# A one-core hybrid decoder layer: a mask moved to a longer-lived pool, decay tiles allocated together and held behind a copy, and another order of the opening's tokens

## The chip, the core and the metric

The kernel runs on one core of a Trainium2 chip. Its time is the device time of one execution in microseconds (us). In the profile PE is the matrix engine, PEld its loading of weights, DVE, ACT and POOL are the vector, scalar and GpSimd engines, and SP issues nearly all DMAs (SPq is its queue). Each engine takes its instructions in a fixed order and waits at the first one whose inputs or buffers aren't ready.

## The reference

One decoder layer works on 1024 tokens of width 1024 in float32. A norm feeds one input projection, whose columns go to two groups of heads that run side by side; their outputs are joined, projected, added to the input, and an MLP follows.

```python
# group A: differential attention, 4 heads, two 64-wide softmax maps per head
s = jnp.einsum('bqhcd,bkhcd->bhcqk', qb, k) * scale
p = jax.nn.softmax(s, axis=-1)
a = p[:, :, 0] - lam * p[:, :, 1]
...
# group B: gated DeltaNet, 4 heads, chunks of 64
g = jnp.cumsum(g, axis=-1)
gdiff = g[..., :, None] - g[..., None, :]
decay = jnp.where(tri, jnp.exp(jnp.where(tri, gdiff, 0.0)), 0.0)
Lmat = jnp.where(strict, jnp.einsum('bhncd,bhnjd->bhncj', k_beta, k) * decay, 0.0)
sol = lax.linalg.triangular_solve(Lmat, rhs, left_side=True, lower=True, unit_diagonal=True)
...
def step(state, inp):      # scanned over the chunks
    v_new = u_c - jnp.einsum('bhcd,bhde->bhce', w_c, state)
    ...
    state = state * jnp.exp(g_last)[..., None, None] + jnp.einsum('bhcd,bhce->bhde', k_dec, v_new)
```

## The kernel before

A float32 matrix product is made of three passes in a narrower format: each operand is split into a high and a low part (hH and hL of the activations, wH and wL of the weights), and PE multiplies high by high, low by high and high by low. ACT makes the high part by a cast, DVE the low part by a subtraction. So every projection step is three matmuls on three neighbouring lines (L305 to L307 for the DeltaNet projections, L1391 to L1393 for the attention's queries and keys).

The work runs in this order.

- **Opening.** The tokens come in transposed, 128 at a time (`xT`, blocks tb of 0 to 7), and the gate projection `z` in two units of columns, u of 0 and 1. Its first blocks take the raw tokens (`z_raw`, L452); later blocks are scaled by their norm first (`z_scale_parts`). For that ACT sums squares, DVE and POOL make a root (`z_root`: nrt, nr), ACT a diagonal matrix (`z_diag`: dg), and PE spreads it over the partitions (`z_spread`: ps_r, L511). The order on all engines is written out by hand here (`manual_schedule`).
- **DeltaNet projections**, in the order keys, queries, values (`dn_proj(1)`, `dn_proj(0)`, `dn_proj(2)`), four heads in two halves each. A half's 24 matmuls end in a bank of a two-bank pool (pj), and ACT copies it away (`cp`, L763), which frees the bank. Weights come in 128x512 pieces (`load_unit`, `wraw`), in two buffers; a buffer is free when ACT has cast it and DVE has subtracted. Beside the keys, `decay(h, hf)` makes the matrix of decays: four ACT products each for rrh and rrl (L832), two matmuls into ps_e (L834, L835), an exponential.
- **Triangular inverses.** `invert()` inverts blocks of 32, and `horner` joins them to blocks of 128, two heads per call, four calls. A call multiplies ps_p (L909), masks it with `blk` into pb (DVE, L912), runs ps_h with 96, 64 and 32 columns (L917), each after what DVE or ACT made of the one before, and scales its result W (DVE, L925).
- **Scan and attention.** From here a planner interleaves the scan over chunks with the attention's projections (ps_qk) and then the attention itself, the output projection and the MLP. The scan reads parked keys and values into `pka` (SP, L1066, four DMAs a chunk), multiplies W by them (ps_A, L1107), applies the result (L1118), updates the state S, and for the second chunk takes the remainder `sr` (DVE, L1073) after a product with S (L1098).

The order of the instructions comes from a scheduler that simulates the program as it is written, except in the opening. Memory comes from pools that are stacked: `sp` lives through the scan, `gp` lies above it and is closed before the scan, whose pool `sb` is then opened in its place. A tile that takes over memory waits for the last reader of what lay there. In the kernel before, `blk` is in `gp`, and its memory lies under the first `pka`.

Of the kernel before, what the change touches and what calls it, by code (L numbers as in the profile page):

```python
# [9 lines left out]
F32 = mybir.dt.float32  # L10
# [8 lines left out]
P = 128  # L19
# [206 lines left out]
def tile_hymba_layer(  # L226
# [161 lines left out]
    def z_load(u, k):  # L388
        nc.sync.dma_start(wz[u][1][k // 2].rearrange("p k c -> p (k c)"), w_z[u, k // 2, :, 0:2 * UC])

    wz = [z_unit() for u in range(2)]
    for tb in range(2):
        xTs[tb] = n1.tile([P, KB, P], F32, tag="xT", name="xT", bufs=6)

    def x_piece(eng, tb, a, b):
        eng.dma_start(xTs[tb][:, a:b, :], x_cols[tb, :, a:b, :])

    z_load(0, 0)
    x_piece(nc.sync, 0, 0, 2)
    x_piece(nc.scalar, 0, 2, 4)  # L400
    z_load(0, 2)
    x_piece(nc.sync, 0, 4, KB)
    z_load(0, 4)
    z_load(0, 6)
    x_piece(nc.sync, 1, 0, KB)
    for k in range(0, KB, 2):
        z_load(1, k)
    dnw4 = n1.tile([P, 4, P], F32, name="dnw4")
# [69 lines left out]

    sums, roots, spreads, diags = {}, {}, {}, {}

    def z_weigh(tb, *at):
        for a, b in zip(at, at[1:]):
            V.tensor_tensor(xTs[tb][:, a:b, :], xTs[tb][:, a:b, :],
                            w1c[:, a:b].unsqueeze(2).broadcast_to([P, b - a, P]), ALU.mult)

    def z_hi(tb, i):
        S.copy(hH[:, cuts[i], tb * P:(tb + 1) * P], xTs[tb][:, cuts[i], :])
# [10 lines left out]
    def z_root(tb):  # L498

        r = roots[tb] = n1.tile([P, 1], F32, name=f"nr{tb}")  # L500
        rstd(r, sums[tb], 1.0 / DM, EPS, n1, "nrt", 1)
# [12 lines left out]
    def z_scale_parts(tb):  # L514
        sl = slice(tb * P, (tb + 1) * P)
        xT, last = xTs[tb], []
        for c in cuts:
            if tb < 2:
                V.tensor_tensor(xT[:, c, :], xT[:, c, :], spreads[tb].unsqueeze(1).broadcast_to([P, 4, P]), ALU.mult)
            else:  # L520
                for k in range(c.start, c.stop):
                    V.scalar_tensor_tensor(xT[:, k, :], xT[:, k, :], w1c[:, k:k + 1], spreads[tb], ALU.mult, ALU.mult)
            last.append(S.copy(hH[:, c, sl], xT[:, c, :]))
        yield
        for c in cuts:
            last.append(V.tensor_tensor(hL[:, c, sl], xT[:, c, :], hH[:, c, sl].bitcast(F32), ALU.subtract))
        yield last

    def z_scale(tb):
        return list(z_scale_parts(tb))[1]  # L530

    ones = gp.tile([P, P], F32, name="ones")
    V.memset(ones, 1.0)
    tri = sp.tile([P, P], F32, name="tri")
    gt_f = gp.tile([P, P], F32, name="gt_f")
    blk = gp.tile([P, P], F32, name="blk")
    caus_f = gp.tile([P, P], F32, name="caus_f")
    G.memset(caus_f, 0.0)
    G.affine_select(caus_f, caus_f, pattern=[[-1, P]], compare_op=ALU.is_ge, fill=-1.0e30,
# [9 lines left out]
    with tc.manual_schedule(engines={T.engine, V.engine, S.engine, G.engine}):  # L549

        pw = pm.tile([P, 512], F32, tag="pm", name="ps_w")
        for i in range(10):
            T.transpose(pw[:, 0:P], ident, ident)
        z_weigh(0, 0, 2, 4)
        z_round(0, 0)
        z_hi(0, 0)
        z_lo(0, 0)
        z_weigh(0, 4, KB)
        z = {(0, 0): z_raw(0, 0, pj, "pj")}
        z_round(0, 1)  # L560
        z_rest(0, 0)
        z_hi(0, 1)
        z_rest(0, 1)
        z_lo(0, 1)
        z_round(0, 2)
        z_rest(0, 2)
        z_weigh(1, 0, 4, KB)
        z_round(0, 3)
        z_rest(0, 3)
        z[1, 0] = z_raw(1, 0, pj, "pj")  # L570
        for i in range(4):
            z_round(1, i)
            z_rest(1, i)
            if i % 2 == 0:
                z_hi(1, i // 2)
        z_square(2)
        z_root(2)
        z_diag(2)
        z_lo(1, 0)
        z_lo(1, 1)  # L580
        z[0, 1] = z_ahead(0, 1, ph, "ph")
        z_spread(2)
        z_square(3)
        z_root(3)
        z_diag(3)
        G.tensor_scalar(dnw4[:, 0], dnw4[:, 0], 0.5, None, ALU.mult)
        G.tensor_copy(dnw4[:, 1:4], dnw4[:, 0:1].broadcast_to([P, 3, P]))
        dnw4 = dnw4.rearrange("p h e -> p (h e)")
        z[1, 1] = z_ahead(1, 1, ph, "ph")
        z_spread(3)  # L590
        z_scale(2)
        z_square(0)
        z_square(1)
        parts = z_scale_parts(3)
        next(parts)
        for tb in range(2):
            z_root(tb)
        next(parts)
        z_square(4)
        z_root(4)  # L600

        pools = {3: (pj, "pj"), 4: (ph, "ph"), 5: (pt_, "pt"), 6: (pj, "pj"), 7: (ph, "ph")}
        z[2, 0] = z_ahead(2, 0, pt_, "pt")
        z_gate(0, 0, z[0, 0], True)
        z_diag(4)
        z[2, 1] = z_mm(2, 1, pt_, "pt")
        z_gate(1, 0, z[1, 0], True)
        z_square(5)
        gates_due = {(3, 0): ((0, 1), (1, 1)), (3, 1): ((2, 0), (2, 1)), (4, 1): ((3, 0), (3, 1)),
                     (5, 0): ((4, 0), (4, 1)), (5, 1): ((5, 0),), (6, 0): ((5, 1),), (6, 1): ((6, 0),),  # L610
                     (7, 0): ((6, 1),), (7, 1): ((7, 0), (7, 1))}
        spread_at = {(3, 0): (4, 1), (3, 1): (5, 3), (4, 1): (6, 1), (5, 0): (7, 3), (5, 1): (0, 3), (6, 0): (1, 3)}
        for tb in range(3, NT):
            for u in range(2):
                nxt, at = spread_at.get((tb, u), (None, 0))
                z[tb, u] = z_mm(tb, u, *pools[tb], nxt, at)
                if nxt is not None:
                    parts = z_scale_parts(nxt)
                    if nxt == 5:
                        z_square(7)  # L620
                    next(parts)
                    if nxt in (4, 5):
                        b = {4: 5, 5: 7}[nxt]
                        z_root(b)
                        z_diag(b)
                    last = next(parts)
                    if nxt == 5:
                        mark = [marks[5], *last]
                for b, v in gates_due.get((tb, u), ()):
                    z_gate(b, v, z[b, v], b < 2)  # L630
                if (tb, u) == (3, 0):
                    z_square(6)
                    z_root(6)
                    z_diag(6)
                if (tb, u) == (3, 1):
                    z_diag(0)
                    z_diag(1)
# [110 lines left out]
    for cp in cps:  # L748
        V.memset(cp[:, 0:3], 0.0)

    def dn_proj(kind):
        for pr in range(2):
            with tc.issue_after(x_last.ins) if kind == 1 and pr == 0 else ExitStack():
                w = load_unit(w_units[4 + 2 * kind + pr])
            for hl in range(2):
                h = 2 * pr + hl
                u = 4 * kind + h
                cp = cps[hl]
                for hf in range(2):
                    ps = pj.tile([P, 512], F32, tag="pj", name="ps_dn")  # L760
                    trn(ps, w, hl * P, hf)
                    b = 512 * hf
                    S.copy(cp[:, 3 + b:3 + b + 512], ps)  # L763
                    y = ta("cy", 2)
                    S.activation(y, cp[:, 3 + b:3 + b + 512], AF.Copy, scale=pv[:, 36 + u:37 + u])  # L765
                    for wi in (2, 1, 0):
                        V.scalar_tensor_tensor(y, cp[:, wi + b:wi + b + 512], pv[:, 12 * wi + u:12 * wi + u + 1],  # L767
                                               y, ALU.mult, ALU.add)
                    if kind == 1:
                        th = ta("cth", 2)  # L770
                        S.activation(th, y, AF.Tanh, scale=0.5)
                        yield h, hf, y, th
                    else:
                        o = ta("cth" if hf else "k2", 2)
                        S.activation(o, y, AF.Silu)
                        yield h, hf, o
# [48 lines left out]
    dts = {}  # L825

    def decay(h, hf):
        rh, rl = ta("rrh", 1, F32R), ta("rrl", 1, F32R)
        for t, col in ((rh, ggh), (rl, ggl)):
            for c in range(4):  # L830
                i = cidx(h, 4 * hf + c)
                S.activation(t[:, c * P:(c + 1) * P], tri, AF.Copy, scale=col[:, i:i + 1])  # L832
        pse = ph.tile([P, 512], F32, tag="ph", name="ps_e")
        T.matmul(pse, gt_r, rh, start=True, stop=False)  # L834
        T.matmul(pse, gt_r, rl, start=False, stop=True)  # L835
        dtm = sa.tile([P, 512], F32, name=f"dtm{h}{hf}")
        S.activation(dtm, pse, AF.Exp)
        G.tensor_tensor(v4(dtm), v4(dtm), bc_mask(tri), ALU.mult)
        dts[h, hf] = dtm

    def invert():

# [12 lines left out]

    lt = {}
    for h, hf, y, th in skew(dn_proj(1)):
        decay(h, hf)
        k2 = ta("k2", 2)
        V.scalar_tensor_tensor(k2, th, 1.0, y, ALU.add, ALU.mult)  # L860
        park(h, hf, 0, k2)
# [1569 lines left out]
```

## Time and profile before

| | |
|---|---|
| median of 3 runs | 1207.59 us (1206.82 to 1209.14) |
| profiled execution | 1208.18 us |
| its span | 1206.5 us, 1.7 us less than its time |
| PE busy | 1195.2 us, 99% of the span |
| DVE, ACT, POOL busy | 854.1, 619.6, 143.0 us |
| mean granted clock of PE | 0.999 |

Rows of a timeline give start, duration, engine, line, operation, tile and inputs, the shape and the count, and in brackets how long the engine had been idle and what ended it. Matmuls overlap, so the cost of one is the distance from its start to the next one's start, not its duration. Rows of windows give the stretch, its length, the busy time and the number of instructions of PE, PEld, DVE, ACT and POOL, the granted clock of PE as a share of full speed, the share of the DMA engines and the GB/s.

### The profile page before, as it was taken

How to read it: one execution, taken by the hardware profiler on the slowest of the kernel's cores; microseconds unless marked ns; L12 is line 12 of the kernel's file. 1: busy time of each engine (PE TensorE's matmuls, PEld its weight loads, DVE VectorE, ACT ScalarE, POOL GpSimd, SP SyncE). 2: the span in 40 equal slices, each digit the busy share in tenths (PEclk: the TensorE clock that was granted, in tenths of full speed). 3: DMA queues.
4: the chain of work that ended last, by engine and by line, in shares of the span. 5: the costliest groups of instructions: out<-in, count | busy, mean ns of one | idle time of the engine just before them, and what ended most of it. 6: DMA issues, size and time to landing. Idle time of an engine off the chain costs nothing.

```text
span 1206.5 us, 17495 instructions
## 1 busy us (share of the span) xinstructions
PE 1195.2 (99%) x6183; PEld 998.0 (83%) x6183; DVE 854.1 (71%) x1655; ACT 619.6 (51%) x1226; POOL 143.0 (12%) x183
## 2 busy tenths in 40 slices
PE   9999999999999999999999999999999999999998
PEld 8978888878888777888888888888888888888887
DVE  6879897656677799886895655456669755786543
ACT  6588553424446666785664544445653333333330
POOL 2423210013322333011100000000000000000000
PEclk9999999999999999999999999999999999999999
DMA  9344654526755766213537443344489555423301
GB/s 352 95 120 122 173 161 88 126 80 217 221 165 156 215 182 187 62 40 116 172 118 249 176 156 125 137 174 174 157 280 386 189 209 194 139 87 105 140 35 70
DMA packets 163966, 191.56 MB, mean 159 GB/s; under 512 B 63160, under 2 KB 119720, under 8 KB 163880
## 3 DMA queue, kind: packets, MB, share of 16 engines
q1 hardware_dynamic: 160136, 180.72, 46.9%
q0 software_dynamic: 3456, 9.60, 2.2%
q8 instruction: 48, 0.79, 0.3%
q14 instruction: 38, 0.31, 0.1%
q10 hardware_dynamic: 288, 0.14, 0.0%
HBM read 129.43 MB, written 60.98 MB: 158 GB/s over the span
## 4 chain that ended last, share of the span: by engine, by line
PE 95%; DVE 1%; ACT 1%; DMA 1%; issue 0%; POOL 0%; SPq 0%; DVEq 0%; ACTq 0%
PE X L2001 5%; PE X L2003 5%; PE X L2002 5%; PE X L2330 4%; PE X L2329 4%; PE X L2328 4%; PE ps_dn L307 3%; PE ps_dn L305 3%; PE ps_dn L306 3%; PE ps_o L1644 3%; PE ps_sc L1551 3%; PE ps_qk L1391 3%; PE Y L2001 3%; PE Y L2003 3%; PE Y L2002 3%; PE ps_qk L1393 2%
## 5 line engine op out<-in xcount | busy, mean ns | idle before, releaser
L1880 ACT CAST hH<-ur 128x1024 fp32r<-128x1024 f32 x56 | 58.9, 1051 | 173.3 <-PE Y L2329 89.4
L1881 DVE TENSOR_TENSOR hL<-ur,hH 128x1024 fp32r<-128x1024 f32 x56 | 68.4, 1222 | 79.3 <-ACT hH L1880 79.3
L1881 DVE TENSOR_TENSOR op<-raw,op 128x1024 fp32r<-128x1024 f32 x48 | 58.7, 1223 | 73.6 <-PE X L2002 40.4
L2328 PE MATMUL X<-hH 128*128 128x512 f32 x224 | 87.1, 389 | 0.0
L2329 PE MATMUL X<-hL,hH 128*128 128x512 f32 x224 | 87.1, 389 | 0.0
L2330 PE MATMUL X<-hH,hL 128*128 128x512 f32 x224 | 87.1, 389 | 0.0
L305 PE MATMUL ps_dn<-hH,wH 128*128 128x512 f32 x192 | 75.9, 395 | 0.5 <-ACT cp L763 0.5
L307 PE MATMUL ps_dn<-hH,wL 128*128 128x512 f32 x192 | 75.3, 393 | 0.0
L306 PE MATMUL ps_dn<-hL,wH 128*128 128x512 f32 x192 | 75.3, 392 | 0.0
L1881 DVE TENSOR_TENSOR hL<-dw,hH 128x1024 fp32r<-128x1024 f32 x56 | 68.1, 1218 | 0.8 <-ACT hH L1880 0.7
L1880 ACT CAST op<-raw 128x1024 fp32r<-128x1024 f32 x48 | 50.4, 1051 | 35.1 <-PE Y L2003 19.9
L1880 ACT CAST hH<-dw 128x1024 fp32r<-128x1024 f32 x56 | 58.6, 1046 | 10.6 <-DMA dw<-in_w_down_dram 4.9
L767 DVE SCALAR_TENSOR_TENSOR cy<-cp,pv,cy 128x512 f32<-128x512 f32 x72 | 58.2, 809 | 6.4 <-ACT cy L765 5.6
L1513 ACT ACTIVATE pexp<-pexp,mx,small 128x128 f32<-128x128 f32 (+7 forms) x64 | 55.1, 863 | 14.7 <-DVE mx L1529 14.6
L1788 PE MATMUL ps_op<-wH,hH 128*128 128x512 f32 x128 | 54.1, 422 | 0.0
L1391 PE MATMUL ps_qk<-hH,wH 128*128 128x512 f32 x128 | 53.0, 414 | 0.0
L1393 PE MATMUL ps_qk<-hH,wL 128*128 128x512 f32 x128 | 50.9, 398 | 0.0
L1392 PE MATMUL ps_qk<-hL,wH 128*128 128x512 f32 x128 | 50.5, 394 | 0.0
L1790 PE MATMUL ps_op<-wH,hL 128*128 128x512 f32 x128 | 50.3, 393 | 0.0
L1789 PE MATMUL ps_op<-wL,hH 128*128 128x512 f32 x128 | 50.0, 391 | 0.0
L2001 PE MATMUL Y<-hH,op 128*128 128x512 f32 x128 | 49.8, 389 | 0.0
L2002 PE MATMUL Y<-hL,op 128*128 128x512 f32 x128 | 49.8, 389 | 0.0
(400 smaller groups left out, 3403.9 us busy)
## 6 DMA issues: line engine op xcount, KB each, us to landing
ur<-ud SPq DMA_DIRECT2D x28, 1024.0 KB, 5.0
raw<-in_w_up_dram SPq DMA_DIRECT2D x32, 512.0 KB, 4.0
dw<-in_w_down_dram SPq DMA_DIRECT2D x32, 512.0 KB, 6.5
wraw<-in_w_units_dram SPq DMA_DIRECT2D x40, 256.0 KB, 3.7
ud<-ua SPq DMA_DIRECT2D x16, 512.0 KB, 4.0
ud<-s SPq DMA_DIRECT2D x16, 512.0 KB, 2.8
pka<-park_d SPq DMA_DIRECT2D x32, 192.0 KB, 4.2
xt<-in_x_dram SPq DMA_DIRECT2D x8, 512.0 KB, 10.3
```

The costliest lines, as they stand in the source:

```text
L305: T.matmul(ps, lh(k), rh(k), start=(k == 0), stop=False)
L306: T.matmul(ps, lh(k), rl(k), start=False, stop=False)
L307: T.matmul(ps, ll(k), rh(k), start=False, stop=(k == n - 1))
L1391: T.matmul(ps, wh[:, k, cs], hH[:, k, sl], start=(k == 0), stop=False)
L1880: S.copy(dst[0], src)
L1881: V.tensor_tensor(dst[1], src, dst[0].bitcast(F32), ALU.subtract)
L2001: T.matmul(ps, op[0][:, k, cs], h[0][:, k, :], start=start and k == 0, stop=False, skip_group_check=True)
L2002: T.matmul(ps, op[0][:, k, cs], h[1][:, k, :], start=False, stop=False, skip_group_check=True)
L2003: T.matmul(ps, op[1][:, k, cs], h[0][:, k, :], start=False, stop=stop and k == 3, skip_group_check=True)
L2328: T.matmul(bank[t], v[0][:, j, sl], v[2][:, j], start=s0, stop=False, skip_group_check=True)
L2329: T.matmul(bank[t], v[0][:, j, sl], v[3][:, j], start=False, stop=False, skip_group_check=True)
L2330: T.matmul(bank[t], v[1][:, j, sl], v[2][:, j], start=False, stop=s1, skip_group_check=True)
```

## The change

1. `blk` is allocated in `sp`, beside the tiles that live through the scan, and no longer in `gp`.
2. All eight decay tiles (`dtm`) are allocated when the first decay is made, ahead of rrh and rrl.
3. The first decay is placed behind the first copy `cp` of the key projection (`issue_after`), and its four low products are made by DVE in place of ACT.
4. In the opening the first half of the first tokens is loaded ahead of the first piece of weights, in one DMA on SP; before, it was two DMAs, one on SP behind those weights and one on ACT's queue. The first weighing by w1c is one DVE instruction in place of two.
5. `z_scale_parts` gives way after each half of a block, so that the root and the diagonal for block 5 stand between the two halves of block 4.

```diff
     wz = [z_unit() for u in range(2)]
-    for tb in range(2):
-        xTs[tb] = n1.tile([P, KB, P], F32, tag="xT", name="xT", bufs=6)
...
-    z_load(0, 0)
-    x_piece(nc.sync, 0, 0, 2)
-    x_piece(nc.scalar, 0, 2, 4)
-    z_load(0, 2)
-    x_piece(nc.sync, 0, 4, KB)
-    z_load(0, 4)
-    z_load(0, 6)
-    x_piece(nc.sync, 1, 0, KB)
+    halves0 = load_xT(0, 2)
+    next(halves0)
+    z_load(0, 0)
+    next(halves0)
+    for k in range(2, KB, 2):
+        z_load(0, k)
+    next(load_xT(1))
...
             last.append(S.copy(hH[:, c, sl], xT[:, c, :]))
-        yield
+            yield
...
-    blk = gp.tile([P, P], F32, name="blk")
+    blk = sp.tile([P, P], F32, name="blk")
...
                     next(parts)
-                    if nxt in (4, 5):
-                        b = {4: 5, 5: 7}[nxt]
-                        z_root(b)
-                        z_diag(b)
+                    if nxt == 4:
+                        z_root(5)
+                        z_diag(5)
+                    next(parts)
+                    if nxt == 5:
+                        z_root(7)
+                        z_diag(7)
...
-                    S.copy(cp[:, 3 + b:3 + b + 512], ps)
+                    copies[kind, h, hf] = S.copy(cp[:, 3 + b:3 + b + 512], ps)
...
     def decay(h, hf):
+        if not dts:
+            dts.update({(a, b): sa.tile([P, 512], F32, name=f"dtm{a}{b}") for a in range(HEADS) for b in range(2)})
...
-                S.activation(t[:, c * P:(c + 1) * P], tri, AF.Copy, scale=col[:, i:i + 1])
+                part = t[:, c * P:(c + 1) * P]
+                if t is rl and (h, hf) == (0, 0):
+                    V.tensor_scalar(part, tri, col[:, i:i + 1], None, ALU.mult)
+                else:
+                    S.activation(part, tri, AF.Copy, scale=col[:, i:i + 1])
...
-        dtm = sa.tile([P, 512], F32, name=f"dtm{h}{hf}")
+        dtm = dts[h, hf]
...
     for h, hf, y, th in skew(dn_proj(1)):
-        decay(h, hf)
+        with tc.issue_after(copies[1, 0, 0].ins):
+            decay(h, hf)
```

What this moves on the engines shows at three places. On ACT, in the first key projection, where the casts wH of the weights, the products rrh and rrl of the first decay and the copies cp meet, there stands before:

```order
L299 CAST wH_1316<-wraw 128x512 x2
L832 ACTIVATE rrh<-tri,gghr 128x128 x4
L832 ACTIVATE rrl<-tri,gglr 128x128 x4
L299 CAST wH_1316<-wraw 128x512
L763 COPY cp_1007<-ps_dn 128x512
L299 CAST wH_1316<-wraw 128x512
L763 COPY cp_1007<-ps_dn 128x512
```

and in the changed kernel:

```order
L299 CAST wH_1319<-wraw 128x512 x3
L762 COPY cp_1005<-ps_dn 128x512
L837 ACTIVATE rrh<-tri,gghr 128x128 x4
L299 CAST wH_1319<-wraw 128x512
L764 ACTIVATE cy<-cp_1005,pv 128x512
L762 COPY cp_1005<-ps_dn 128x512
```

The first copy now stands ahead of the first decay's products, and behind the third cast. On PE the two matmuls of the first decay (ps_e) move from right behind ps_g to behind fifteen matmuls of the next half's projection.

On PE at the scan's opening, where the fourth `horner` call (ps_p, ps_h) meets the scan's first products (ps_A from pka), there stands before:

```order
L1393 MATMUL ps_qk<-hH,wL_2995 128x512
L917 MATMUL ps_h<-W,pb 32x32 x8
L909 MATMUL ps_p<-gb_1730,lt 128x96 x4
L909 MATMUL ps_p<-gb_1732,lt 128x96 x4
L917 MATMUL ps_h<-W,pb 96x96 x8
L917 MATMUL ps_h<-W,pb 64x64 x8
L1107 MATMUL ps_A<-pka,W 128x128
L917 MATMUL ps_h<-W,pb 32x32 x4
L1107 MATMUL ps_A<-pka,W 128x128
L917 MATMUL ps_h<-W,pb 32x32 x4
L1107 MATMUL ps_A<-pka,W 128x128 x2
```

and in the changed kernel, at the scan's first products and, some forty rows later, at its products with the state S:

```order
L1398 MATMUL ps_qk<-hH,wL_2993 128x512
L1112 MATMUL ps_A<-pka,W 128x128 x4
L1396 MATMUL ps_qk<-hH,wH_2992 128x512
L1397 MATMUL ps_qk<-hL,wH_2992 128x512
L1398 MATMUL ps_qk<-hH,wL_2993 128x512
L1396 MATMUL ps_qk<-hH,wH_2992 128x512
L1397 MATMUL ps_qk<-hL,wH_2992 128x512
L922 MATMUL ps_h<-W,pb 32x32 x8
L1398 MATMUL ps_qk<-hH,wL_2993 128x512
L1123 MATMUL ps_A<-sy,pka 128x128 x4
```

```order
L1103 MATMUL ps_A<-S_3219,pka 128x128
L1103 MATMUL ps_A<-S_3222,pka 128x128
L922 MATMUL ps_h<-W,pb 64x64 x8
L922 MATMUL ps_h<-W,pb 32x32 x8
L1103 MATMUL ps_A<-S_3236,pka 128x128
L1103 MATMUL ps_A<-S_3245,pka 128x128
```

The first products of the scan come in one piece and ahead of the fourth call, whose last two steps now stand between the products with S, right ahead of the eighteen ps_qk and the remainder's product that follow there in both kernels.

On SP at the start, where the pieces of the gate's weights (wraw) and of the tokens (xT) are loaded, there stands before:

```order
L389 DMA wraw<-in_w_z_dram 128x520
L396 DMA xT<-in_x_cols_dram 128x256
L389 DMA wraw<-in_w_z_dram 128x520
L396 DMA xT<-in_x_cols_dram 128x512
L389 DMA wraw<-in_w_z_dram 128x520 x2
L396 DMA xT<-in_x_cols_dram 128x1024
```

and in the changed kernel:

```order
L382 DMA xT<-in_x_cols_dram 128x512
L389 DMA wraw<-in_w_z_dram 128x520
L382 DMA xT<-in_x_cols_dram 128x512
L389 DMA wraw<-in_w_z_dram 128x520 x3
L382 DMA xT<-in_x_cols_dram 128x1024
```

The block of tokens for tb of 1 (128x1024) keeps its place behind all four pieces of the first unit's weights.

More of the change, by code (lines that the diff above doesn't have):

```diff
@@ L391, in tile_hymba_layer @@
     wz = [z_unit() for u in range(2)]
-    for tb in range(2):
-        xTs[tb] = n1.tile([P, KB, P], F32, tag="xT", name="xT", bufs=6)
-    def x_piece(eng, tb, a, b):
-        eng.dma_start(xTs[tb][:, a:b, :], x_cols[tb, :, a:b, :])
+    halves0 = load_xT(0, 2)
+    next(halves0)
     z_load(0, 0)
-    x_piece(nc.sync, 0, 0, 2)
-    x_piece(nc.scalar, 0, 2, 4)
-    z_load(0, 2)
-    x_piece(nc.sync, 0, 4, KB)
-    z_load(0, 4)
-    z_load(0, 6)
-    x_piece(nc.sync, 1, 0, KB)
+    next(halves0)
+    for k in range(2, KB, 2):
+        z_load(0, k)
+    next(load_xT(1))
     for k in range(0, KB, 2):
@@ L479, in tile_hymba_layer, with z_weigh @@
     sums, roots, spreads, diags = {}, {}, {}, {}
[L481 to L484, printed above, removed]
+    def z_weigh(tb, i):
+        V.tensor_tensor(xTs[tb][:, cuts[i], :], xTs[tb][:, cuts[i], :],
+                        w1c[:, cuts[i]].unsqueeze(2).broadcast_to([P, 4, P]), ALU.mult)
     def z_hi(tb, i):
@@ L529, in z_scale @@
     def z_scale(tb):
-        return list(z_scale_parts(tb))[1]
+        return list(z_scale_parts(tb))[-1]
     ones = gp.tile([P, P], F32, name="ones")
@@ L553, in tile_hymba_layer @@
             T.transpose(pw[:, 0:P], ident, ident)
-        z_weigh(0, 0, 2, 4)
+        z_weigh(0, 0)
         z_round(0, 0)
@@ L557, in tile_hymba_layer @@
         z_lo(0, 0)
-        z_weigh(0, 4, KB)
+        z_weigh(0, 1)
         z = {(0, 0): z_raw(0, 0, pj, "pj")}
@@ L566, in tile_hymba_layer @@
         z_rest(0, 2)
-        z_weigh(1, 0, 4, KB)
+        z_weigh(1, 0)
+        z_weigh(1, 1)
         z_round(0, 3)
@@ L621, in tile_hymba_layer @@
                     next(parts)
-                    if nxt in (4, 5):
-                        b = {4: 5, 5: 7}[nxt]
-                        z_root(b)
-                        z_diag(b)
+                    if nxt == 4:
+                        z_root(5)
+                        z_diag(5)
+                    next(parts)
+                    if nxt == 5:
+                        z_root(7)
+                        z_diag(7)
                     last = next(parts)
@@ L749, in tile_hymba_layer @@
         V.memset(cp[:, 0:3], 0.0)
+    copies = {}
     def dn_proj(kind):
@@ L835, in decay @@
         T.matmul(pse, gt_r, rl, start=False, stop=True)
-        dtm = sa.tile([P, 512], F32, name=f"dtm{h}{hf}")
+        dtm = dts[h, hf]
         S.activation(dtm, pse, AF.Exp)
         G.tensor_tensor(v4(dtm), v4(dtm), bc_mask(tri), ALU.mult)
-        dts[h, hf] = dtm
     def invert():
```

## The prediction

> **What bounds the kernel now.** I read the page's first part, then PE's waits, then the clock in windows, then the timelines of the three places. The page shows which engine sets the end:
>
> ```profile
> span 1206.5 us, 17495 instructions
> PE 1195.2 (99%) x6183; PEld 998.0 (83%) x6183; DVE 854.1 (71%) x1655; ACT 619.6 (51%) x1226; POOL 143.0 (12%) x183
> ```
>
> PE lacks 11.3 us of the span. The change removes no matmul, so it can win only PE's idle time and what PE loses at a lower clock. PE's waits, as total, times and longest in us:
>
> ```profile
> PE ps_A L1107 <- DMA pka<-park_d: 1.6, 3, 1.0
> PE ps_z L452 <- DVE xT L483: 1.1, 1, 1.1
> PE ps_r L511 <- ACT dg L506: 0.8, 1, 0.8
> ```
>
> Windows about the longest of these (length, then PE, PEld, DVE, ACT and POOL busy, PE's granted clock, DMA share, GB/s), and for comparison one at the first decay:
>
> ```profile
> 264.50:267.90 3.40, 2.20 (x22) 1.55 (x22) 1.60 (x4) 0.74 (x3) 0.00 (x0) 1.00 0.81 243
> 268.00:270.00 2.00, 1.93 (x6) 1.65 (x7) 0.68 (x1) 1.33 (x3) 0.00 (x0) 0.50 0.64 239
> 270.00:272.00 2.00, 2.00 (x11) 1.71 (x10) 0.71 (x2) 0.84 (x2) 0.00 (x0) 0.66 0.46 122
> 69.95:73.35 3.40, 2.23 (x9) 1.43 (x9) 1.67 (x4) 3.40 (x9) 0.00 (x0) 1.00 0.24 67
> ```
>
> Behind the waits for pka the granted clock is halved: 0.50 to 270, and the 0.66 of the next row means half up to about 271.4 and full from there, some 3.4 us in all. The 3.4 us ahead of it had PE busy for 2.20. A like stretch at the first decay had 2.23 and kept its clock. So 1.2 us of idle in 3.4 us is near the point where the clock falls.
>
> **The scan's opening (blk to the long-lived pool).** SP's queue and the mask's last use:
>
> ```profile
> 244.27 1.34 SPq L1274 DMA_DIRECT2D L<-ss_d  x2
> 262.03 1.99 SPq L1066 DMA_DIRECT2D pka<-park_d  x4
> 261.44 0.56 DVE L912 TENSOR_TENSOR pb<-ps_p,blk 128x384 f32<-128x384 f32 x1 [0.32 <-PE ps_p L909]
> ```
>
> SP issues nothing from about 245.6 on, and pka goes out at 262.03, right when the last masking ends at 262.00: pka lies where blk lay. With blk elsewhere pka follows L at about 245, lands before the scan wants it, and the 1.6 us of waits go. PE in that stretch:
>
> ```profile
> 250.05 1.52 PE L917 MATMUL ps_h<-W,pb 128*96 128x96 f32 x16
> 251.35 0.47 PE L1393 MATMUL ps_qk<-hH,wL 128*128 128x512 f32 x1
> 255.86 1.15 PE L917 MATMUL ps_h<-W,pb 128*64 128x64 f32 x16
> 256.94 0.50 PE L1391 MATMUL ps_qk<-hH,wH 128*128 128x512 f32 x1
> 258.52 0.69 PE L917 MATMUL ps_h<-W,pb 128*32 128x32 f32 x16
> 259.38 2.02 PE L909 MATMUL ps_p<-gb,lt 128*128 128x96 f32 x16 [0.16 <-ACT W L923]
> 261.24 3.05 PE L917 MATMUL ps_h<-W,pb 128*96 128x96 f32 x32
> 268.07 0.80 PE L1107 MATMUL ps_A<-pka,W 128*128 128x128 f32 x2 [1.04 <-DMA pka<-park_d]
> 279.72 1.05 PE L1098 MATMUL ps_A<-S,pka 128*128 128x128 f32 x8
> 280.53 0.48 PE L1391 MATMUL ps_qk<-hH,wH 128*128 128x512 f32 x1
> 284.74 1.05 PE L1107 MATMUL ps_A<-sr,W 128*128 128x128 f32 x8
> L1391 PE MATMUL ps_qk<-hH,wH x21: 389/393/774, 256.9 to 284.1; 128*128 128x512 f32 x21
> ```
>
> From 256.94 to 284.74, 27.80 us, both kernels have the same matmuls. What are they worth without waits? ps_qk: 21 steps of three passes, 63 matmuls; the last 18 take 280.53 to 284.74, 4.21, so 0.234 each and 14.7 in all. Three blocks of ps_A (from pka, sy and S) at 279.72 to 280.53: 0.81 each, 2.4. The fourth call's ps_p 1.86 (259.38 to 261.24); its ps_h of 96 and 64 columns as in the third call, 1.30 and 1.08; ps_h of 32 columns of both calls at 0.86, 1.7. Sum 23.1, so 4.7 us are lost. The half clock takes PE's part of it, 268.07 to 271.4, 3.3 us at half speed: 1.64. The other 3.0 are waits, those for pka and small ones in the fourth call.
>
> The new order brings waits of its own. DVE's work that stands ahead of the remainder sr:
>
> ```profile
> 259.36 1.29 DVE L925 TENSOR_TENSOR W<-W,vsc 128x512 f32<-128x512 f32 x2 [2.31 <-ACT W L923]
> 279.08 0.72 DVE L1311 STREAM_TRANSPOSE tq<-ps_qk 128x512 f32<-128x512 f32 x1 [0.65 <-ACT ps_qk L1308]
> 279.83 0.69 DVE L1317 TENSOR_REDUCE part<-tq 128x16 f32<-128x512 f32 x1
> 280.81 0.35 DVE L1073 SCALAR_TENSOR_TENSOR sr<-ps_A,neg_eg,pka 128x128 f32<-128x128 f32 x1 [0.29 <-PE ps_A L1098]
> 283.19 0.35 DVE L1073 SCALAR_TENSOR_TENSOR sr<-ps_A,neg_eg,pka 128x128 f32<-128x128 f32 x1
> ```
>
> Since the fourth call's last step now stands between the products with S, its scaling of W (1.29), the transposition (0.72), the reduction (0.69) and the stretch of the four sr (280.81 to 283.54, 2.73) follow one another: 5.4, with about 0.5 for ACT's copy ahead of them 5.9. Beside them PE has half a block of ps_A (0.4) and the eighteen ps_qk (4.21), so ps_A from sr waits 1.3. Bounds: 0, if the scheduler's other work on DVE slips behind them, and 5.9, if nothing covers. Its ps_h of 32 columns, right behind that of 64, waits for ACT's copy, some 0.3 (between 0.16, the wait in the row at 259.38, and 0.5). I take waits of 3.0 - 1.6 = 1.4 us won, and a single wait of 1.3 beside dense ps_qk is near the bound of 1.2 yet spread over a window that is otherwise full; I take the half clock here as gone, 1.64.
>
> **The first decay (behind the first copy, low products by DVE).** PE, ACT, DVE and the weights' DMAs there:
>
> ```profile
> 69.98 0.49 PE L834 MATMUL ps_e<-rrh,gt_r 128*128 128x512 f32 x1
> 71.15 0.49 PE L835 MATMUL ps_e<-rrl,gt_r 128*128 128x512 f32 x1 [0.67 <-ACT rrl L832]
> 72.14 0.50 PE L305 MATMUL ps_dn<-hH,wH 128*128 128x512 f32 x1 [0.50 <-ACT cp L763]
> 69.84 1.26 ACT L832 ACTIVATE rrl<-tri,gglr 128x128 fp32r<-128x128 f32 x4
> 71.00 0.60 ACT L299 CAST wH<-wraw 128x512 fp32r<-128x512 f32 x1
> 71.51 0.58 ACT L763 COPY cp<-ps_dn 128x512 f32<-128x512 f32 x1
> 66.66 0.69 DVE L300 TENSOR_TENSOR wL<-wraw,wH 128x512 fp32r<-128x512 f32 x1 [1.26 <-ACT wH L299]
> DMA to landing us min/median/max: 3.2/3.5/3.6
> ```
>
> Before, PE waits 0.67 for rrl and 0.50 for the copy. The change takes rrh and rrl from ahead of the copy, but the third cast still stands ahead of it. That cast reads a buffer that DVE frees at 67.35; its DMA needs 3.2 to 3.6 us, so it lands at 70.6 to 71.0. Cast (0.51 to the next start) and copy (0.6) then let ps_dn start at 71.7 to 72.1: at most 0.4 sooner. The two ps_e (0.23 each, as for a ps_qk) still come, now behind fifteen ps_dn, where rrh and DVE's four products are long done: 0.46. So the place costs between +0.06 and +0.46; I take +0.3 and keep -0.7 (the copy not held by the cast: 1.17 of waits less 0.46) as the lower end. Allocating the decay tiles early moves addresses only; no row shows PE waiting for one, so 0.
>
> But the idle becomes one piece: PE has nothing from the end of ps_g at 69.98 to about 71.9, 1.9 us in place of 0.67 and 0.50. That is over the 1.2 us at which the scan's clock fell, in the midst of dense matmuls. A half clock of 3.4 us would cost 1.64 here too, as PE is full behind it. It needs most of the 1.9 us to lie in one window, so it isn't certain; I give it six in ten, and the forecast includes it.
>
> The Trainium skill ("TensorE: Matmul & The Clock Gate", Part 1) says that the clock falls after an idle window of about 3.4 us that runs freely. The length agrees with the 3.4 us here; that the window must be idle doesn't agree with the 2.20 us of PE's work in the window ahead of the fall.
>
> **The opening.**
>
> ```profile
> 5.00:10.00 5.00, 5.00 (x15) 4.10 (x16) 4.23 (x8) 2.82 (x5) 0.00 (x0) 1.00 1.03 357
> 40.27 0.39 PE L427 MATMUL ps_z<-wH,hH 128*128 128x260 f32 x1 [0.51 <-DVE zg L465]
> 38.99 0.20 ACT L694 ACTIVATE ea<-alog 128x4 f32<-128x4 f32 x1 [0.67 <-DMA alog<-in_A_log_dram]
> ```
>
> The DMA engines are full (1.03), and the bytes up to the second token block stay the same, so the order of two pieces wins little: one DMA fewer, -0.15, with bounds of -0.5 and +0.4, half of PE's first wait of 1.1 either way. The diagonal for block 5 comes earlier, so PE's 0.8 for dg goes; but PE then reaches 40.27 sooner, and there it waits through the gate for ACT, which waits for alog's DMA, which no part of the change moves. So that 0.8 is paid again: 0 (at best -0.8).
>
> **The sum**, against the profiled execution: 1208.18 - 0.15 (opening) + 0.3 (first decay) + 1.64 (its half clock) - 1.4 (scan's waits) - 1.64 (scan's half clock) = 1206.9 us. The execution lies 0.6 above the median of the runs. Faster or slower by over 0.2%, about what a measurement of this kernel can tell from no change, means 2.4 us: below 1205.2 or above 1210.0.
>
> **Rivals.**
> - The clock holds at the first decay, since the 1.9 us are split over two windows or the bound lies higher: 1206.9 - 1.64 = 1205.3, and with the lower end of the opening below 1205.2. For it: 1.17 us of idle was borne there. Against it: 1.2 was too much in the scan. By the skill's rule, too, the clock would hold.
> - The first decay pays: the copy isn't held by the cast, -0.7 in place of +0.3, and the clock holds: 1204.3. Against it: the cast's DMA can't be issued before 67.35.
> - Slower: DVE becomes the bound at the remainder. If the fourth call comes so late that none of its 5.9 us is covered, the scan has waits of 6.2 in place of 3.0, and the clock falls within them as before: 1208.18 - 0.15 + 0.3 + 1.64 + 3.2 = 1213.2. It decides from about 3 us of wait at sr on, with both half clocks kept (1210.0). Against it: the eighteen ps_qk stand ahead of that product in both kernels.
> - The mask doesn't set pka free, because another reader of that memory is as late: then only the decay and the opening count, 1208.3, or 1210.0 with its half clock. For it: nothing in the order tells which tile lies under pka next.
>
> **How the numbers follow.** Forecast 0.43, clock holds 0.20, decay pays 0.08, DVE the bound 0.09, pka not free 0.12, something unseen 0.08. Faster: half of the second case, the third, a tenth of the first's lower edge and half of the unseen: 0.28. Slower: the fourth, a quarter of the fifth, a bit of the unseen: 0.13. The rest, 0.59, is within 0.2%. The range goes from the case where the decay pays, 1204.1, to the fifth with its half clock, 1209.9.
>
> **What the profile of the changed kernel would show.** pka issued at about 245, and no wait of ps_A for it; a granted clock of 1.00 in 264 to 272; ps_A from sr waiting some 1.3 for DVE; one wait of about 1.9 of ps_dn for cp near 70, none for rrl, and 0.50 in some windows right behind it; the wait for dg gone, and that for zg longer by as much. Wrong would be: pka issued after 260, a wait at sr over 3, a full clock behind the first decay, or ps_dn started before 71.

## The result, and the profile after

The changed kernel takes 1205.52 us (median of 9 runs, 1204.68 to 1207.54) against 1207.60 of the kernel before (9 runs beside it, 1206.82 to 1210.55). By the medians 2.1 us are gone. The ratio is 0.9979, with an interval of 0.9970 to 0.9988; here and below it is an estimate over the runs, not the quotient of the two medians. The forecast was 1206.9, within a range of 1204.1 to 1209.9. Its profiled execution takes 1205.46, 2.7 less than that of before. One run among all the experiments, 1320.33 us at a mean granted clock of 0.851, lies far outside the rest and is in no median or ratio below.

The page's first rows, and then all waits of PE over 0.3 us:

```profile
span 1203.5 us, 17479 instructions
PE 1193.6 (99%) x6183; PEld 997.0 (83%) x6183; DVE 853.8 (71%) x1658; ACT 617.4 (51%) x1222; POOL 144.7 (12%) x183
```

```profile
PE ps_w L545 <- POOL ident masks.py:199: 1.5, 1, 1.5
PE ps_dn L305 <- ACT cp L762: 1.1, 1, 1.1
PE ps_z L420 <- DVE zg L458: 0.9, 1, 0.9
PE ps_A L1112 <- DVE sr L1078: 0.9, 1, 0.9
PE ps_z L445 <- DVE xT L475: 0.6, 1, 0.6
PE ps_o L1649 <- ACT at L1638: 0.4, 1, 0.4
PE ps_z L445 <- DMA wraw<-in_w_z_dram: 0.4, 1, 0.4
```

The waits for pka, for dg and for rrl are gone. In their place stand a wait for sr, a longer one for cp, a longer one for zg and one for the opening's weights.

**The scan's opening.** SP's queue, PE's timeline and the windows that had the half clock before:

```profile
245.37 2.21 SPq L1071 DMA_DIRECT2D pka<-park_d  x4
```

```profile
256.65 0.50 PE L1396 MATMUL ps_qk<-hH,wH 128*128 128x512 f32 x1
258.15 1.05 PE L1112 MATMUL ps_A<-pka,W 128*128 128x128 f32 x8
281.10 1.16 PE L1112 MATMUL ps_A<-sr,W 128*128 128x128 f32 x8 [0.86 <-DVE sr L1078]
```

```profile
264.50:267.90 3.40, 3.40 (x25) 3.09 (x24) 2.48 (x6) 0.00 (x0) 0.00 (x0) 1.00 0.99 231
268.00:270.00 2.00, 2.00 (x11) 1.64 (x10) 0.00 (x0) 0.35 (x1) 0.00 (x0) 1.00 0.92 332
270.00:272.00 2.00, 2.00 (x21) 1.85 (x20) 0.63 (x2) 0.83 (x2) 0.54 (x1) 1.00 1.04 376
```

pka goes out right behind L, 16.7 us sooner than before, and no ps_A waits for it. The same matmuls that took 27.80 us take 24.45 (256.65 to 281.10). One wait is left, 0.86 for sr, and the clock stays at 1.00.

**The first decay.** PE (one row of the kernel before first, then the changed kernel), then ACT and the clock of the changed kernel:

```profile
69.76 0.39 PE L721 MATMUL ps_g<-gg,ones 128*128 128x32 f32 x2
```

```profile
69.96 0.39 PE L718 MATMUL ps_g<-gg,ones 128*128 128x32 f32 x2
71.42 0.50 PE L305 MATMUL ps_dn<-hH,wH 128*128 128x512 f32 x1 [1.07 <-ACT cp L762]
70.26 0.62 ACT L299 CAST wH<-wraw 128x512 fp32r<-128x512 f32 x1 [2.21 <-DMA wraw<-in_w_units_dram]
70.79 0.58 ACT L762 COPY cp<-ps_dn 128x512 f32<-128x512 f32 x1
69.95:73.35 3.40, 2.33 (x13) 1.90 (x12) 1.36 (x5) 3.09 (x8) 0.00 (x0) 1.00 0.33 105
```

ACT sat idle for 2.21 us ahead of the third cast while the finished projection waited to be copied behind it. PE has one piece of 1.07 us without work, and its clock stays at 1.00. From ps_g to the ps_qk behind the third call's 64 columns (69.96 to 256.65) the changed kernel needs 186.69 us, the kernel before 187.18 (69.76 to 256.94): 0.49 less.

**The opening.** In these two executions ps_g comes 0.20 later than before. The first gate projections in the kernel before (first row) and the changed one (busy time, mean ns of one, waits), and then the gate's wait in the changed one:

```profile
L452 PE MATMUL ps_z<-wraw,xT 128*128 128x260 f32 x32 | 9.3, 453 | 1.1 <-DVE xT L483 1.1
```

```profile
L445 PE MATMUL ps_z<-wraw,xT 128*128 128x260 f32 x32 | 10.5, 499 | 1.0 <-DVE xT L475 0.6 <-DMA wraw<-in_w_z_dram 0.4
40.48 0.39 PE L420 MATMUL ps_z<-wH,hH 128*128 128x260 f32 x1 [0.91 <-DVE zg L458]
```

The same 32 matmuls take 46 ns more each on average. By the clock records of the two traces full clock began 11.20 us behind the start here and 8.52 in the kernel before, so more of these matmuls ran ahead of it (rows of windows print 1.00 there for want of a record). Most of that is gone again by the gate, where PE waits for zg. So in the pair of profiles: +0.2, -0.5, and -3.35 in the scan's opening make -3.64 by the first ps_A from sr (284.74 to 281.10). The spans differ by 3.0; the 0.6 that are given back behind the scan's opening come in pieces of 0.3 and less, and I didn't follow them.

### The profile page after: what moved, and what is told of

The parts are those of the page before. It is cut to its first block, busy times and chain, and to the rows that moved or that the text cites. A ratio compares the mean times of both kernels' runs of the same rounds, so it can differ in the third digit from the quotient of the medians.

```text
span 1203.5 us, 17479 instructions
## 1 busy us (share of the span) xinstructions
PE 1193.6 (99%) x6183; PEld 997.0 (83%) x6183; DVE 853.8 (71%) x1658; ACT 617.4 (51%) x1222; POOL 144.7 (12%) x183
## 4 chain that ended last, share of the span: by engine, by line
PE 96%; DVE 1%; ACT 1%; DMA 1%; issue 0%; POOL 0%; SPq 0%; DVEq 0%; ACTq 0%
PE X L2008 5%; PE X L2006 5%; PE X L2007 5%; PE X L2334 4%; PE X L2335 4%; PE X L2333 4%; PE ps_dn L305 3%; PE ps_dn L306 3%; PE ps_dn L307 3%; PE ps_sc L1556 3%; PE Y L2008 3%; PE ps_o L1649 3%; PE Y L2006 3%; PE Y L2007 3%; PE ps_qk L1396 2%; PE ps_op L1793 2%
```

## The experiments

Two theories of the gain stood against each other after the result. A: the mask carries nearly all of it, through pka. B: the three places carry like parts. A second pair was on the clock. C: the half clock goes to whatever window has idle enough, the first decay's as well as the scan's. D: it belongs to the scan alone. The first four kernels make one part of the change each.

**The mask alone.**

```diff
-    blk = gp.tile([P, P], F32, name="blk")
+    blk = sp.tile([P, P], F32, name="blk")
```

> Only the mask is moved to the long-lived pool. Theory A (the scan's opening carries the gain): no wait for pka, one wait of 0.8 to 1.3 for sr, granted clock 1.00 about 268, the stretch from the first ps_qk behind the third call's 64 columns to the first ps_A from sr 24.4 us in place of 27.8; time 1.7 to 3.3 below the kernel before, ratio 0.9973 to 0.9986. Theory B (the gain comes from the three places in like parts): under 1.0 us, ratio over 0.9992.

Measured 1206.46 us, ratio 0.9982 (0.9974 to 0.9991). pka goes out at 247.79, the waits for it are gone and one of 0.9 for sr is there; the stretch takes 24.49 us (259.07 to 283.56). Windows of its profile, two neighbouring ones at the first decay and one in the scan, and behind them the first ps_e:

```profile
69.98:73.39 3.41, 2.22 (x10) 1.39 (x9) 1.20 (x4) 3.41 (x10) 0.00 (x0) 1.00 0.24 81
73.39:76.80 3.41, 3.41 (x9) 2.68 (x9) 1.62 (x4) 3.38 (x8) 0.00 (x0) 0.50 0.55 159
264.00:268.00 4.00, 4.00 (x28) 3.59 (x27) 3.31 (x8) 2.00 (x5) 0.54 (x1) 1.00 0.72 201
70.50 0.50 PE L834 MATMUL ps_e<-rrh,gt_r 128*128 128x512 f32 x1
```

The part does what theory A said, and its interval shuts out B's 0.9992, if barely. But the half clock stands now at the first decay, where this kernel is the kernel before unchanged. There it follows the same two waits, for rrl and for cp, that were borne in the profile before. So one profile with a half clock and one without differ by 1.6 us whatever the change is. That speaks for C.

**The decay's part alone** (tiles together, behind the first copy, low products by DVE, as in the diff above).

> Only the decay's part (tiles together, behind the first copy, low products by DVE). Theory A: one wait of some 1.1 for cp in place of 0.67 and 0.50, the two ps_e paid later, in all 0.4 us less, ratio 0.9997; the waits for pka and a half clock at the scan stay. Theory B: 0.7 to 1.0 us less, ratio 0.9992 to 0.9994. If the clock falls behind the first decay, as forecast: 1.3 to 1.9 us more, ratio 1.0010 to 1.0015.

Measured 1207.15 us (11 runs), ratio 0.9988 (0.9979 to 0.9998): faster, by the ratio more than either theory gave, with both inside the interval. PE at the first decay, its waits for pka, and the scan's window:

```profile
71.30 0.50 PE L305 MATMUL ps_dn<-hH,wH 128*128 128x512 f32 x1 [1.21 <-ACT cp L765]
256.50 0.50 PE L1399 MATMUL ps_qk<-hH,wH 128*128 128x512 f32 x1
PE ps_A L1115 <- DMA pka<-park_d: 0.7, 2, 0.5
264.00:268.00 4.00, 3.43 (x29) 2.66 (x30) 1.61 (x4) 1.41 (x5) 0.00 (x0) 1.00 0.93 291
268.00:272.00 4.00, 4.00 (x22) 3.18 (x21) 3.46 (x8) 2.10 (x5) 0.54 (x1) 1.00 0.61 160
```

pka still goes out behind the mask, yet this execution waits 0.7 for it, not 1.6, and the scan's clock holds. So neither the size of that wait nor the half clock behind it is fixed: both differ where the scan's code is the same. The profiles of the next two kernels, which also have the mask in its old place, agree: they wait 1.4 and 1.1 for pka, and their granted clock is 1.00 from 262 to 274. The clock also held behind the single wait of 1.21.

**The order of the tokens alone** (tokens and weights on SP, one weighing).

> Only the opening's order of tokens and weights on SP and one weighing in place of two. Theory A: -0.2 to +0.2 us by the time of the first decay, ratio 0.9998 to 1.0002. Theory B: 0.4 to 0.8 us less, as PE starts 0.44 sooner, ratio 0.9994 to 0.9997.

Measured 1208.75 us, ratio 1.0002 (0.9993 to 1.0010): nothing that can be told. Its profile, too, has the half clock behind the first decay (the window ahead of it, and one within it), and none behind its waits for pka:

```profile
69.43:72.84 3.41, 2.24 (x11) 1.50 (x10) 1.19 (x4) 3.41 (x10) 0.00 (x0) 1.00 0.35 106
74.00:76.00 2.00, 2.00 (x7) 1.54 (x6) 0.63 (x3) 1.97 (x5) 0.00 (x0) 0.50 0.74 196
PE ps_A L1100 <- DMA pka<-park_d: 1.4, 3, 0.8
```

**The halves alone** (`z_scale_parts` gives way after each half).

> Only the scaling that gives way after each half. Theory A: the wait for dg (0.8) goes and comes back at the gate, where DVE's zg is what PE waits for in both kernels: 0 to -0.1 us, ratio 1.0000. Theory B: the wait for dg is won, 0.8 us less, ratio 0.9993.

Measured 1206.65 us, ratio 0.9992 (0.9983 to 1.0001). The wait for dg (0.8) is gone. The wait at the gate, 0.51 before, and the one for pka are these:

```profile
PE ps_z L427 <- DVE zg L465: 0.7, 1, 0.7
PE ps_A L1111 <- DMA pka<-park_d: 1.1, 2, 0.9
```

Only 0.2 of the 0.8 comes back, and ps_g stands at 69.02 in place of 69.76; theory B is nearer. The interval reaches just past 1, so the time alone doesn't settle it; in this pair of profiles the waits speak for it. The four ratios make -0.0036 together, the whole change -0.0021; with intervals of nearly 0.001 to either side of each that isn't a contradiction. Between A and B: the mask is the largest part, -0.0018, but the decay's part by its interval and the halves by their waits aren't nothing, so neither theory holds whole.

**Two kernels with one part left out**, on one chip: the changed kernel without the order of the tokens, and without the decay's part. A kernel with all but the mask's move was not run.

> The changed kernel with the tokens and weights of the opening in the old order (mask, decay and halves alone). If the order of tokens is worth nothing, as it was alone: the time of the changed kernel, ratio to the kernel before 0.9979, lowest run 1204.6 to 1204.9. If it costs what the later full clock of the opening cost in the changed kernel's profile: 0.3 us faster, ratio 0.9976.

Measured 1205.11 us, ratio 0.9973 (0.9963 to 0.9983). The order of the tokens is worth nothing, or costs a few tenths.

> The changed kernel without the decay's part. Theory C (the half clock is drawn by two waits of 0.67 and 0.50 in one clock window just as by pka's): lowest run 1205.2 to 1205.4, 0.6 above the changed kernel's lowest, and some runs 1.6 above that, with the half clock behind the first decay; median 1206.3, ratio 0.9984. Theory D (the half clock belongs to the scan alone): all runs within 0.8 of the lowest, median 1205.6, ratio 0.9978.

Measured 1205.71 us, ratio 0.9984 (0.9975 to 0.9993). Of its 11 runs eight lie at 1204.16 to 1205.76 and three at 1207.34 to 1208.29, a group of its own some 2 above, as theory C has it; but its lowest runs came 1 us lower than expected, and the median lies nearer to theory D's 1205.6. Its profile has no half clock, so where the three lost it isn't shown. Against the whole change's 0.9979 the decay's part would be worth 0.0005, 0.6 us, less than either interval can tell.

**The copy first.** The third cast holds the copy, and the copy holds PE. The casts of that unit are only needed two projections later, so its loads are put behind the copy (with mask, decay and halves, and the old order of tokens):

```diff
+            behind_of = {(1, 0): x_last, (1, 1): copies.get((1, 0, 0))}.get((kind, pr))
-            with tc.issue_after(x_last.ins) if kind == 1 and pr == 0 else ExitStack():
+            with tc.issue_after(behind_of.ins) if behind_of else ExitStack():
                 w = load_unit(w_units[4 + 2 * kind + pr])
```

> The kernel with mask, decay and halves, and the weights of the second pair of heads loaded behind the first copy, so that no cast stands ahead of it on ACT. Theory C: no wait for cp (1.1 less), no window with over 0.9 us of idle left behind the opening, so no half clock: lowest run 1203.4 to 1203.7, all runs within 1.0 of it, median 1203.9, ratio 0.9966. Theory D: the same 1.1 less, and the same spread of runs as in the changed kernel: median 1204.4, ratio 0.9970.

Measured 1203.74 us, ratio 0.9966 (0.9954 to 0.9978), as theory C has it; its 6 runs lie at 1202.98 to 1205.15, 2.2 apart in place of the 1.0 expected. Its span, its waits, and ACT's copy:

```profile
span 1201.2 us, 17489 instructions
```

```profile
PE ps_w L553 <- POOL ident masks.py:199: 1.5, 1, 1.5
PE ps_z L452 <- DVE xT L483: 1.2, 2, 1.0
PE ps_A L1120 <- DVE sr L1086: 0.8, 1, 0.8
PE ps_z L427 <- DVE zg L465: 0.7, 1, 0.7
PE ps_o L1657 <- ACT at L1646: 0.4, 1, 0.4
67.21 0.59 ACT L770 COPY cp<-ps_dn 128x512 f32<-128x512 f32 x1 [4.13 <-PE ps_dn L307]
```

The copy runs as soon as the projection is done, and PE waits for nothing at the first decay. On another chip all parts of the change with this one more were measured:

> The changed kernel, all parts, with the second pair's weights behind the first copy. No wait for cp: 1.1 to 1.6 us less than the changed kernel on the same chip; if the order of tokens is worth nothing, within 0.4 us of the 1203.74 of the kernel without that part.

1203.83 us, ratio 0.9967 (0.9954 to 0.9979), and beside it the changed kernel as it is:

> The changed kernel once more, beside the two others on one chip: ratio to the kernel before 0.9979 as at first; wait for cp about 1.1, for sr 0.9, no half clock, or one behind the first decay in a run that is 1.6 longer.

1205.48 us, ratio 0.9978 (0.9969 to 0.9987). So by the medians of one chip each the copy is worth 1.65 us here (its wait is 1.45 in this profile) and 1.37 in the kernel without the order of tokens (1205.11 against 1203.74, with a wait of 1.24): its wait and little more. All five runs with the copy first lie below all eleven of the changed kernel on that chip.

**How long a wait the clock bears.** The changed kernel with its first copy made three times, and twice:

```diff
+                    for _ in range(2 if (kind, h, hf) == (1, 0, 0) else 0):
+                        S.copy(cp[:, 3 + b:3 + b + 512], ps)
                     copies[kind, h, hf] = S.copy(cp[:, 3 + b:3 + b + 512], ps)
```

> The changed kernel with its first copy cp made three times over, so that PE's wait at the first decay grows from 1.1 to some 2.7 us. If over 1.2 us of idle in a window of 3.4 us halves the clock, each execution has it there: 1.6 + 1.6 us more, median 1208.5 to 1209.0, ratio 1.0002. If an idle window of 3.4 us is needed: 1.6 us more alone, median 1207.1, granted clock 1.00 in 70 to 78, ratio 0.9992.

Measured 1209.17 us, ratio 1.0010 (1.0002 to 1.0019), nearer the first case and above it. The wait came out at 3.5, since the fourth cast went between the copies, and the clock was halved for two windows:

```profile
PE ps_dn L305 <- ACT cp L764: 3.5, 1, 3.5
68.04:71.45 3.41, 1.41 (x9) 1.14 (x7) 1.79 (x7) 1.36 (x3) 0.00 (x0) 1.00 0.41 130
71.45:74.86 3.41, 1.90 (x5) 1.51 (x6) 1.02 (x3) 3.38 (x9) 0.00 (x0) 0.50 0.41 146
74.86:78.28 3.42, 3.42 (x10) 2.65 (x9) 2.26 (x5) 2.69 (x6) 0.00 (x0) 0.50 0.03 13
```

> The changed kernel with its first copy made twice, so that PE's single wait at the first decay is about 2.2 us, a little over the 1.9 that the prediction reckoned with. If that much idle among wide matmuls halves the clock in most executions: 1.1 + 1.2 us over the changed kernel on the same chip, and a window of 0.50 behind 71. If the clock holds: 1.1 over it, granted clock 1.00 there.

Measured 1208.35 us, ratio 1.0000 (0.9991 to 1.0008), 2.9 above the changed kernel on that chip for 1.0 to 1.4 more of wait (2.5 against its 1.1 and 1.5). The difference, some 1.5 to 1.9, fits a half clock's price, and the profile shows the half clock; below it, the changed kernel's second profile, where a single wait of 1.45 kept its clock:

```profile
69.43:72.84 3.41, 0.98 (x7) 0.79 (x5) 1.56 (x5) 2.23 (x5) 0.00 (x0) 1.00 0.27 97
72.84:76.26 3.42, 3.38 (x8) 2.71 (x9) 1.30 (x4) 3.40 (x7) 0.00 (x0) 0.50 0.44 153
```

```profile
71.61 0.50 PE L305 MATMUL ps_dn<-hH,wH 128*128 128x512 f32 x1 [1.45 <-ACT cp L762]
69.01:72.42 3.41, 1.96 (x12) 1.59 (x10) 1.80 (x7) 1.96 (x6) 0.00 (x0) 1.00 0.39 123
```

## Why the prediction was right or wrong

**The scan's opening: right.** I reckoned 1.4 of waits and 1.64 of half clock won, 3.04, and a new wait of 1.3 for sr; the profiles show 3.35 and 0.86. That the half clock goes was right for this pair of profiles. What I missed is that it wasn't a fixed part of the kernel before. The three profiles with the mask in its old place and no half clock there need 25.60 (decay's part), 25.88 (halves) and 26.84 us (tokens) for the same 167 matmuls. Against 24.45 the move wins 1.2 to 2.4 in them, and 3.35 where the clock fell. That is likely why the medians differ by 2.1 and the profiles by 2.7.

**The first decay: wrong in size and sign.** The step that failed is "at most 0.4 sooner", with +0.3 for the place. It took the landing of the third cast's weights at 70.6 to 71.0. They landed at 70.26, since DVE freed the buffer sooner and the DMA was as quick as the quickest, so ps_dn started 1.46 us behind ps_g in place of 2.38. That the cast ahead of the copy would hold it was right: ACT waits 2.21 for the weights and PE 1.07 for the copy, and the kernel with the copy first shows it by removing it. The place wins 0.4 to 0.5 (0.38 with the part alone, from 69.70, where its ps_g stands, to 256.50). The lower end, -0.7 for the case that the cast doesn't hold the copy, was mis-sized too: it is 1.17 of waits less 0.46 for the two ps_e behind other matmuls, and leaves out that alone between two waits each had held PE for its 0.49. With these 0.98 it is -1.7; the kernels with the copy first, 1.4 and 1.65 below those without on top of the 0.4 to 0.5, are in that case.

**The half clock at the first decay: wrong.** The step is "over the 1.2 us at which the scan's clock fell". The wait was 1.07, not 1.9, so the profile doesn't test the price; the kernels with repeated copies do. The full clock there was among the prediction's own signs of being wrong. A single wait of 1.45 in one window of 3.4 us kept the clock, one of 2.5 lost it. So 1.2 us of idle is no bound: among the wide matmuls of the first decay it lost the clock in two profiles (mask alone, tokens alone) and kept it in the kernel before. The rival that the clock holds, 1205.3, is the case that came, 0.2 from the measured time. That is in part luck: it expected a wait of 1.9 to be borne, and the wait was shorter. By the rule of the Trainium skill ("TensorE: Matmul & The Clock Gate", Part 1) it takes an idle window of about 3.4 us. That doesn't agree with these runs: 2.5 us of idle, with PE busy for 0.98 in the window, were enough.

**The opening: small, and wrong in its reason.** I gave -0.15 and 0 for dg, as alog's DMA would bind at the gate. In the changed kernel ACT didn't wait for alog; PE waited 0.9 for zg, and with the halves alone 0.2 of dg's 0.8 came back. The tokens' order is worth nothing, as reckoned.

**The sum.** 1208.18 - 0.15 + 0.3 + 1.64 - 1.4 - 1.64 = 1206.9 lies 1.5 above the profiled execution. The +1.64 that didn't come and the +0.3 that was -0.5 made it 2.4 too high. About 1.0 went the other way: the opening cost 0.2 in place of winning 0.15, 0.6 were given back behind the scan's opening, and the time is 2.0 longer than the span in place of 1.7, against 0.3 more won in the scan's opening. So errors covered each other, and that the time lies within the range is in part luck. It is 0.2% below the kernel before, at the edge between the two chances. Two slips change little: the cases named for the ends of the range sum to 1204.3 and 1210.0, not 1204.1 and 1209.9, and the parts named for the chance of faster to 0.26, not 0.28.

## What to carry to other kernels

Look at whose memory a tile takes over, not only at what it reads: a small mask in the wrong pool held a queue for 16 us. When a copy frees the bank that the next matmul needs, see what stands ahead of it on its engine; a prefetch that nobody needs yet can hold everything. Before a half clock in one profile is counted as the price of a wait, look at it in several executions: here the same code lost the clock at one place, at another, or nowhere.

## What the runs showed of the hardware that wasn't expected

The half clock came for 3.41 us at a time (twice in a row with three copies). Single waits of 1.07, 1.21, 1.24 and 1.45 were borne; the last had PE busy for just 1.96 of 3.41. Behind several short waits the clock fell with PE busy for 2.20 (the scan in the profile before), 2.22 and 2.24 of 3.41, and held with this (the first decay in the profile before):

```profile
69.96:73.37 3.41, 2.24 (x9) 1.44 (x9) 1.67 (x4) 3.41 (x9) 0.00 (x0) 1.00 0.24 65
```

So PE's busy time doesn't tell. Two things in the traces tell more. First, the clock falls on a fixed beat: from its beginning to its fall the full clock lasted 259.41 us in the profile before, 64.85 with the mask or the tokens alone and 61.44 with repeated copies, which is 76, 19 and 18 times 3.413. The beat lies differently in each execution (full clock began 7.99 to 11.40 us behind the start in the thirteen profiles), and so the same wait falls into one window or across two.

Second, counting the 128x512 matmuls in such a window at the first decay (0.227 us each, those at the edges in part; 15 fit) puts the profiles in one order. The clock fell behind 2.0 (copy twice), 3.9 (three times), 4.8 (mask alone) and 5.5 (tokens alone). It held behind 5.8 (the changed kernel's second profile), 6.8, 6.9 (the kernel before) and all above. The kernel before and the mask alone have nearly the same window, 69.96 and 69.98 on, and the same waits; but with the mask alone the first ps_e comes at 70.50 in place of 69.98, and the window holds 4.8 such matmuls in place of 6.9. This order was found afterwards, in eleven profiles at one place. The four narrow ps_g aren't counted, and other windows with few wide matmuls but many narrow ones held, so it is no general bound.
